# The adaLN shift as a bias per output column, in place of a term in h

## The chip, the cores and the metric

The kernel runs on one core of a Trainium2 chip. The metric is the device time of one execution in microseconds (us), median of three runs, less is better. The engines are named as in the profile: PE is TensorE, PEld its weight loads, DVE is VectorE, ACT is ScalarE, POOL is GpSimd, SP is SyncE, which issues the DMA transfers.

## What is computed

One layer of a bidirectional hybrid encoder over 2048 tokens of 1024 channels:

```python
mod = silu(c) @ ada_w + ada_b
shift, scale, gate = split(mod, 3)
h = rms_norm(x, norm_w) * (1.0 + scale) + shift
proj = h @ w_in                     # 1024 -> 3088 columns
u_a, z_a, qkv, z_b, beta_fb, alpha_fb = split(proj)
# u_a: state-space group, then a gated linear unit, times silu(z_a)
# qkv: centred conv of 5 taps, silu, gated delta rule in both directions, times silu(z_b)
out = x + gate * (concat(y_a, y_b) @ w_out)     # then a final rms_norm
```

The shift is one vector for all tokens, so `h @ w_in` is `(h - shift) @ w_in` plus one constant for each output column.

## The kernel before

Tokens lie in four blocks of 512 (b or tb), channels in eight slices of 128 (k). h is kept transposed, as two float16 halves hhi and hlo of h times a power of two; the factor that undoes it is ih. Columns of w_in are taken in jobs of 128: `order` lists four u jobs (numbers 0 to 3, NU = 4), ZA0 to ZA2, the narrow job ab (16 columns: beta and alpha), K0 to K3, Q0 to Q3, and then V0, ZA3, V1, ZB0, V2, ZB1, V3, ZB2, ZB3. A weight is split into halves wh and wl with a power of two of its own: `w_max` squares it on ScalarE with a running sum and adds that up with a matmul against ones; `w_cut` makes scale and inverse iv on VectorE (`pow2_root`), then wh on ScalarE and wl on VectorE. A product (`gemm`) of one job and one block is 24 matmuls of 512 columns, three for each k.

Both stages that the change touches are under a manual schedule: each engine gets its instructions in the order of the program text. Nothing is reordered, and an instruction that waits holds up what stands behind it on its engine.

**The start** (lines 250 to 500) makes the modulation, h and the u jobs. Scale comes first: acc is the weighted sum of eight rows blocks of ada_w, and `mod_sum` adds it up over partitions on TensorE. Block 0 of h is made without the shift, with its own factor ih0 (line 378), and the four u products of block 0 run on it, kept in four PSUM banks. Meanwhile the shift's weighted sum runs on VectorE (`shift_add`) and, for the last two rows, on GpSimd (line 412); `mod_sum(0, ...)` follows in the middle of product 3. Then `h_scale` takes a new factor from scale and shift together, and `h_part` makes block 1 of h with the shift:

```python
A.activation(out=hf, in_=src, func=AF.Identity, scale=aS[:, k:k + 1], bias=shS[:, k:k + 1])
P.tensor_scalar(out=hhi[:, k, sl], in0=hf, scalar1=1.0, scalar2=1.0, op0=ALU.mult, op1=ALU.mult)
V.tensor_tensor(out=hlo[:, k, sl], in0=hf, in1=hhi[:, k, sl], op=ALU.subtract)
```

What block 0 lacks is added to u only: 96 matmuls of one column (line 438) multiply the four u weights with the shift, in halves shh and shl, and the evacuation of block 0 gets the result as a bias. The loop over blocks 1 to 3 (line 465) interleaves the u products with the next block's h: squares and root of x, its scaling, four turns (transposes by TensorE, `h_turn`) per slot and `h_part`. In block 3 the slots for the next h are used to make block 0's h again, from xk, with the shift (line 481). There too the first projection job's weight is prepared.

**The projection jobs** (line 986 on): `job` runs four products, each followed by an evacuation by ScalarE (a z with Silu, or raw for the conv) and by `tick`, which issues what became due: taps and conv of earlier blocks, sums, turns, and a piece of `s5_side`, the state-space branch with its tables. Under the first product the next weight's Square is issued, under the second its small matmul, under the third and fourth its cut. `ab_job` runs its four blocks in four column groups of TensorE at once, and prepares K0's weight in one go behind them, with no tick between. PSUM has two banks for products (gm), three each for pt and sq. The stages behind the jobs are not touched.

Of the kernel before, what the change touches and what calls it, by code (L numbers as in the profile page):

```python
# [9 lines left out]
F32 = mybir.dt.float32  # L10
# [13 lines left out]
KT = D // 128  # L24
# [16 lines left out]
def block(ctx, tc, x, c, ada_w, ada_b, norm_w, w_in, conv_w,  # L41
# [131 lines left out]
    ih = hpool.tile([128, 1], F32, name="ih")  # L173
    cw = s5t.tile([128, 12, 5], F32, name="cw")
# [20 lines left out]
    def w_max(i):  # L195
# [5 lines left out]
        m, ma, s, iv = [sp.tile([128, 1], F32, tag=f"w{j}", name=f"w{j}", bufs=6) for j in range(4)]  # L201
        wh, wl = [pools["wp", i < NU].tile([128, KT, order[i][1]], F16, tag=t, name=t) for t in ("wh", "wl")]
        A.activation(out=wl.bitcast(BF16), in_=ws, func=AF.Square, accum_out=m)
        wprep[i] = [None, ma, s, iv, wh, wl]
# [6 lines left out]
    def w_cut(i):  # L211
# [3 lines left out]
        ps, ma, s, iv, wh, wl = wprep[i]  # L215
        ws = wraw[i]
        pow2_root(ps, ma, s, iv)
        if i >= NU:
            V.tensor_tensor(out=iv, in0=iv, in1=ih, op=ALU.mult)
# [4 lines left out]
        wprep[i] = (wh, wl, iv)  # L224
# [5 lines left out]
    def w_done(i):  # L230
        w = wprep[i][0:3]
        if i < NU:
            V.tensor_tensor(out=w[2], in0=w[2], in1=ih, op=ALU.mult)
        return w
# [15 lines left out]
    with ExitStack() as p0:  # L250
# [134 lines left out]
        ss = x_square(x1)  # L385
        first = []
        iv0 = small("iv0", NU)
# [7 lines left out]
        first.append(gemm(wprep[0], 0))  # L395
        next(cuts[2])
        next(cuts[2])
# [32 lines left out]
        for k in range(3):  # L430
            h_part(1, k, turned[k])
# [1433 lines left out]
```

## Time and profile before

| | us |
|---|---|
| median of three runs | 1396.05 (1393.25 to 1398.34) |
| the profiled execution: own time | 1399.54 |
| its span | 1397.8 |
| PE busy | 1283.2 (92%) |
| DVE busy | 1000.4 (72%) |
| POOL, ACT busy | 703.7, 672.1 |
| mean granted clock of TensorE, as a share of the full one | 0.959 |

The profile is of one execution. Busy time of PE counts overlapping matmuls, whose ends are modelled, so the step from start to start says more than the duration of a row. The full clock of TensorE is 2.4 GHz, its lower level 1.2.

### The profile page before, as it was taken

To read this page: it belongs to the slowest core of one execution; us is meant where nothing else is said; L and a number is where in the kernel's file an instruction comes from. 1 tells how busy PE (TensorE), PEld (TensorE's weight loads), DVE (VectorE), ACT (ScalarE), POOL (GpSimd) and SP (SyncE) were. 2 spreads that over 40 slices of the span, in tenths; PEclk is the share of its full clock that TensorE was granted. 3 is DMA by queue.
4 is the path that set the end of the run, shared out by engine and by line. 5 is a ranking of instruction groups with operands and counts; after the bars stand their busy time and mean duration, and the time that the engine had idled before them with its cause. 6 is when DMAs were issued, how large, how long until landed. Compare 5 with 4: busy or idle time off the path is not lost.

```text
span 1397.8 us, 26533 instructions
## 1 busy us (share of the span) xinstructions
PE 1283.2 (92%) x9936; PEld 902.9 (65%) x9936; DVE 1000.4 (72%) x2095; ACT 672.1 (48%) x1348; POOL 703.7 (50%) x680
## 2 busy tenths in 40 slices
PE   2879897898999999999998789999999988998997
PEld 2445343354665555555554679999998877887885
DVE  4636479877765899889865677888888555865664
ACT  4445321444654555344446566777666423432332
POOL 3214223655541478878731765656653235654443
PEclk9789998999999999999999899999999999999998
DMA  9445342222457434353525423444435487686533
GB/s 313 169 93 180 96 83 84 66 80 83 117 170 186 134 113 144 91 163 100 150 74 150 147 77 116 152 145 138 132 111 197 144 289 276 226 309 211 181 111 108
DMA packets 255280, 206.43 MB, mean 148 GB/s; under 512 B 88496, under 2 KB 206256, under 8 KB 255152
## 3 DMA queue, kind: packets, MB, share of 16 engines
q1 hardware_dynamic: 255152, 204.75, 47.5%
q8 instruction: 78, 1.28, 0.4%
q14 instruction: 50, 0.41, 0.1%
HBM read 133.38 MB, written 73.33 MB: 148 GB/s over the span
## 4 chain that ended last, share of the span: by engine, by line
PE 70%; DVE 16%; DMA 4%; issue 3%; ACT 2%; POOL 2%; SPq 1%; DVEq 0%; POOLq 0%; ACTq 0%
PE gm L33 38%; PE sq L33 16%; PE pt L33 12%; DVE sq L1035 3%; DVE w L510 1%; DVE tm L510 1%; DVE xs L939 1%; PE pt L1079 1%; DMA of<-o_d 1%; DVE t L510 1%; DVE wl L223 1%; PE sq L1752 1%; DMA xt<-in_x_dram 1%; DMA ay_d<-ytx 1%; DVE pb L1423 0%
## 5 line engine op out<-in xcount | busy, mean ns | idle before, releaser
L33 PE MATMUL gm<-hhi,wh 128*128 128x512 f16 (+1 forms) x784 | 294.3, 392 | 14.7 <-ACT wh L221 8.2
L33 PE MATMUL gm<-hhi,wl 128*128 128x512 f16 (+1 forms) x784 | 293.1, 390 | 8.8 <-DVE wl L223 8.8
L33 PE MATMUL gm<-hlo,wh 128*128 128x512 f16 (+1 forms) x784 | 293.3, 391 | 0.0
L33 PEld LDWEIGHTS <-wh 128*128 128x128 f16 (+1 forms) x1664 | 154.0, 101 | 200.6 <-issue 25.3
L33 PEld LDWEIGHTS <-wl 128*128 128x128 f16 (+1 forms) x832 | 79.7, 100 | 106.7 <-DVE wl L223 11.4
L1019 ACT ACTIVATE raw<-gm,w 128x512 f32<-128x512 f32 x48 | 33.1, 690 | 177.6 <-PE gm L33 177.6
L510 POOL TENSOR_TENSOR w<-w,w 128x512 f32<-128x512 f32 x32 | 50.1, 1575 | 83.3 <-DVE w L510 83.3
L33 PE MATMUL gm<-yh,gwh 128*128 128x256 f32 x256 | 80.4, 314 | 6.4 <-ACT yh L778 5.4
L1035 DVE SCALAR_TENSOR_TENSOR sq<-raw,cw,sq 128x512 f32<-128x512 f32 x96 | 72.6, 756 | 3.4
L33 PE MATMUL gm<-yl,gwh 128*128 128x256 f32 x256 | 73.7, 288 | 0.7 <-POOL yl L779 0.7
L1774 POOL TENSOR_TENSOR r<-r,xt 128x512 f32<-128x512 f32 x32 | 41.4, 1295 | 63.5 <-DVE r L1773 31.0
L33 PE MATMUL gm<-yh,gwl 128*128 128x256 f32 x256 | 72.9, 285 | 0.0
L1035 DVE SCALAR_TENSOR_TENSOR sq<-raw,cw,cv 128x512 f32<-128x512 f32 x48 | 50.7, 1057 | 29.3 <-ACT cv L1027 28.7
L1444 ACT ACTIVATE Y<-pt 128x512 f16<-128x512 f32 x96 | 58.0, 604 | 27.1 <-PE pt L33 26.4
L33 PE MATMUL sq<-S,kq 128*128 128x128 f32 x480 | 64.1, 287 | 0.0
L33 PEld LDWEIGHTS sq<-S,kq 128*128 128x128 f32 x480 | 61.7, 201 | 2.0
L1005 ACT ACTIVATE z<-gm,w 128x512 f32<-128x512 f32 x32 | 22.0, 688 | 84.6 <-PE gm L33 49.7
L1423 DVE CAST_PREDICATED pb<-msk,pt 128x512 f16<-128x512 int8 x80 | 56.9, 714 | 6.6 <-PE pt L33 5.4
L939 DVE TENSOR_TENSOR_SCAN xs<-c,w 128x255 f32<-128x255 f32 x64 | 61.1, 1013 | 0.6 <-POOL w L510 0.6
L33 PE MATMUL pt<-Y,nh 128*128 128x64 f16 (+1 forms) x896 | 56.5, 198 | 5.4 <-DVE Y L1431 5.1
L320 POOL TENSOR_SCALAR hhi<-hf 128x512 f16<-128x512 f32 x32 | 30.0, 957 | 55.0 <-ACT hf L318 47.9
L1445 ACT ACTIVATE YT<-pt 128x512 f16<-128x512 f32 x96 | 57.3, 597 | 0.0
(456 smaller groups left out, 3529.8 us busy)
## 6 DMA issues: line engine op xcount, KB each, us to landing
xt<-in_x_dram SPq DMA_DIRECT2D x25, 512.0 KB
ws<-in_w_in_dram SPq DMA_DIRECT2D x24, 512.0 KB
aw<-in_ada_w_dram SPq DMA_DIRECT2D x24, 512.0 KB
kq<-kT_d SPq DMA_DIRECT2D x32, 256.0 KB
kq<-qT_d SPq DMA_DIRECT2D x32, 256.0 KB
kt<-kt_d SPq DMA_DIRECT2D x32, 256.0 KB
vt<-vt_d SPq DMA_DIRECT2D x32, 256.0 KB
out_dram<-r SPq DMA_DIRECT2D x16, 512.0 KB
```

Source lines behind the costliest of these rows:

```text
L33: nc.tensor.matmul(out, lhsT, rhs, start=start, stop=stop)
L223: V.scalar_tensor_tensor(out=wl, in0=ws, scalar=s, in1=wh, op0=ALU.mult, op1=ALU.subtract)
L320: P.tensor_scalar(out=hhi[:, k, sl], in0=hf, scalar1=1.0, scalar2=1.0, op0=ALU.mult, op1=ALU.mult)
L510: (e or V).tensor_tensor(out=o, in0=a, in1=b, op=op)
L939: V.tensor_tensor_scan(out=o, data0=m1, data1=v, initial=0.0, op0=ALU.mult, op1=ALU.add)
L1005: A.activation(out=z, in_=ps, func=AF.Silu, scale=iv)
L1019: A.activation(out=raw[:, 2 + tb * 512:2 + (tb + 1) * 512], in_=ps, func=AF.Copy, scale=iv)
L1035: V.scalar_tensor_tensor(out=cv if j == 4 else ps, in0=raw[:, o + j:o + j + 512], scalar=cw[:, i12, j:j + 1], in1=cv if j == 1 else ps, op ...
L1423: V.copy_predicated(out=cols(PB[d][li], b, d), mask=mb, data=pp.rearrange("p t (n b) -> p t n b", b=b))
L1444: A.activation(out=cols(Y[d], b, d), in_=pa.rearrange("p t (n b) -> p t n b", b=b), func=AF.Copy)
L1445: A.activation(out=cols(YT[d], b, 1 - d), in_=pb.rearrange("p t (n b) -> p t n b", b=b), func=AF.Copy)
L1774: P.tensor_tensor(out=r[:, ns], in0=r[:, ns], in1=xt[:, ns], op=ALU.add)
```

## The change

The shift is kept out of h altogether, in every block. `h_part` becomes two instructions, hhi straight from the source on ScalarE and hlo on VectorE, with no use of GpSimd; block 0 isn't made again, and h's factor comes from scale alone, so it is there from the beginning. Each job instead gets a bias per column, from `w_bias`: 24 matmuls of one column of the weight's halves with the shift's (three for each k), and an evacuation that undoes weight's and shift's factors (ib, a second product beside iv). In a job it is issued behind the first product and ahead of its evacuation; in ab it is 96 matmuls, 24 for each of the four column groups, and four evacuations.

In the start the six u products of block 0 and of jobs 0 and 1 in block 1 are evacuated without a bias into xk (`u_raw`). The shift is summed up between them; squares, root and scaling of block 2 come ahead of its last step. The four u jobs' biases follow product (1,1), and GpSimd adds them to the six kept u (`u_add`), which are stored then.

```diff
+
+    ish = hpool.tile([128, 1], F32, name="ish")
+    sh = [hpool.tile([128, KT], F16, name=n) for n in ("shh", "shl")]
...
@@ -212,26 +215,33 @@
 
         if i >= len(order):
             return
-        ps, ma, s, iv, wh, wl = wprep[i]
+        ps, ma, s, iv, ib, wh, wl = wprep[i]
         ws = wraw[i]
         pow2_root(ps, ma, s, iv)
         if i >= NU:
+            V.tensor_tensor(out=ib, in0=iv, in1=ish, op=ALU.mult)
             V.tensor_tensor(out=iv, in0=iv, in1=ih, op=ALU.mult)
         yield
         A.activation(out=wh, in_=ws, func=AF.Copy, scale=s)
         yield
         V.scalar_tensor_tensor(out=wl, in0=ws, scalar=s, in1=wh, op0=ALU.mult, op1=ALU.subtract)
-        wprep[i] = (wh, wl, iv)
+        wprep[i] = (wh, wl, iv, ib)
 
     def whole(g):
         for _ in g:
             pass
 
...
-    def w_done(i):
-        w = wprep[i][0:3]
-        if i < NU:
-            V.tensor_tensor(out=w[2], in0=w[2], in1=ih, op=ALU.mult)
-        return w
+    def w_bias(w, n, rows=(0,)):
+
+        ps = bank("pt")
+        for k in range(KT):
+            for a, b, j in ((0, 0, 0), (0, 1, 1), (1, 0, 2)):
+                for r in rows:
+                    mm(nc, ps[r:r + n, 0:1], w[a][:, k, :], sh[b][:, k:k + 1], k + j == 0, k == KT - 1 and j == 2)
+        wb = sp.tile([128, 1], F32, tag="wb", name="wb", bufs=NU)
+        for r in rows:
+            A.activation(out=wb[r:r + n], in_=ps[r:r + n, 0:1], func=AF.Copy, scale=w[3][r:r + n])
+        return wb
...
         def h_part(b, k, src):
-            hf = hp.tile([128, 512], F32, tag="hf", name="hf", bufs=4)
-            A.activation(out=hf, in_=src, func=AF.Identity, scale=aS[:, k:k + 1], bias=shS[:, k:k + 1])
             sl = slice(b * 512, (b + 1) * 512)
-            P.tensor_scalar(out=hhi[:, k, sl], in0=hf, scalar1=1.0, scalar2=1.0, op0=ALU.mult, op1=ALU.mult)
-            V.tensor_tensor(out=hlo[:, k, sl], in0=hf, in1=hhi[:, k, sl], op=ALU.subtract)
+            A.activation(out=hhi[:, k, sl], in_=src, func=AF.Copy, scale=aS[:, k:k + 1])
+            V.scalar_tensor_tensor(out=hlo[:, k, sl], in0=src, scalar=aS[:, k:k + 1], in1=hhi[:, k, sl],
+                                   op0=ALU.mult, op1=ALU.subtract)
...
-        s_0, ih0, s_h = [small(n) for n in ("s_0", "ih0", "s_h")]
-        h_scale(bd, s_0, ih0, "h0")
-        aS0, aS, shS = [small(n, KT) for n in ("aS0", "aS", "shS")]
-        V.tensor_scalar(out=aS0, in0=aT, scalar1=s_0, scalar2=None, op0=ALU.mult)
+        s_h, s_s = small("s_h"), small("s_s")
+        h_scale(bd, s_h, ih, "h")
+        aS, shS = small("aS", KT), small("shS", KT)
+        V.tensor_scalar(out=aS, in0=aT, scalar1=s_h, scalar2=None, op0=ALU.mult)
         cuts = {i: w_cut(i) for i in range(1, NU)}
-
         for k in range(KT):
-            A.activation(out=hhi[:, k, 0:512], in_=xk[:, k], func=AF.Copy, scale=aS0[:, k:k + 1])
-            V.scalar_tensor_tensor(out=hlo[:, k, 0:512], in0=xk[:, k], scalar=aS0[:, k:k + 1], in1=hhi[:, k, 0:512],
-                                   op0=ALU.mult, op1=ALU.subtract)
+            h_part(0, k, xk[:, k])
...
-        ss = x_square(x1)
-        first = []
-        iv0 = small("iv0", NU)
+        raws = {}
...
-        first.append(gemm(wprep[0], 0))
-        next(cuts[2])
-        next(cuts[2])
-        shift_add(0, 1)
+        def u_raw(b, ct):
+
+            if b == 0:
+                iv, ib = wprep[ct][2:4]
+                V.tensor_copy(out=ib, in_=iv)
+                V.tensor_tensor(out=iv, in0=iv, in1=ih, op=ALU.mult)
+            u_out(b, ct, gemm(wprep[ct], b), None)
+
+        def u_add(b, ct):
+            ur = raws.pop((b, ct))
+            P.tensor_scalar(out=ur, in0=ur, scalar1=ub[ct], scalar2=1.0, op0=ALU.add, op1=ALU.mult)
+            u_store(b, ct, ur)
+
+        def u_store(b, ct, ur):
+            nc.sync.dma_start(out=u_d[ct * 128:(ct + 1) * 128, :, b * 64:(b + 1) * 64], in_=ur)
+
+        def u_out(b, ct, ps, bias):
+
+            ur = (xk[:, 4 * b + ct].rearrange("p (t r) -> p t r", t=T) if bias is None else
+                  up.tile([128, T, 64], F32, tag="u", name="u"))
+            ps = ps.rearrange("p (r t) -> p t r", t=T)
+            if bias is None:
+                A.activation(out=ur, in_=ps, func=AF.Copy, scale=wprep[ct][2])
+                raws[b, ct] = ur
+            else:
+                A.activation(out=ur, in_=ps, func=AF.Identity, scale=wprep[ct][2], bias=bias)
+                u_store(b, ct, ur)
+
         whole(cuts[2])
-        first.append(gemm(wprep[1], 0))
-        whole(w_max(3))
+        ss = x_square(x1)
+        u_raw(0, 0)
+        mx = w_max(3)
+        next(mx)
         rs = x_root(ss)
         for j in range(4):
             x_scale(x1, rs, j, (A, P)[j % 2])
-        next(cuts[3])
-        next(cuts[3])
+        u_raw(0, 1)
+        whole(mx)
+        whole(cuts[3])
...
+        u_raw(0, 2)
+        shift_add(0, 1)
+        for k in range(0, 4):
+            h_part(1, k, h_turn(x1, k, turns[k % 2]))
         shift_add(2, 3)
-        whole(cuts[3])
+        u_raw(0, 3)
+        for k in range(4, KT):
+            h_part(1, k, h_turn(x1, k, turns[k % 2]))
+        xs_ = {2: x_load(2)}
         shift_add(4, 5)
 
...
-        first.append(gemm(wprep[2], 0, "sq"))
-        turned = [h_turn(x1, k, t) for k, t in enumerate(("pt", "pt", "sq"))]
-        first.append(bank("sq"))
-        gemm_part(first[3], wprep[3], 0, range(4))
+        u_raw(1, 0)
+        ss = x_square(xs_[2])
         mod_sum(0, [acc, aws[6]])
-        gemm_part(first[3], wprep[3], 0, range(4, KT))
-        xs_ = {2: x_load(2)}
+        rs = x_root(ss)
+        for j in range(4):
+            x_scale(xs_[2], rs, j, V)
...
-        V.tensor_tensor(out=bd, in0=bd, in1=bs_, op=ALU.add)
-        h_scale(bd, s_h, ih, "h")
-        V.tensor_scalar(out=aS, in0=aT, scalar1=s_h, scalar2=None, op0=ALU.mult)
-        V.tensor_scalar(out=shS, in0=modc[:, 0:8], scalar1=s_h, scalar2=None, op0=ALU.mult)
-        sh = [hp.tile([128, KT], F16, name=n, bufs=1) for n in ("shh", "shl")]
+        h_scale(bs_, s_s, ish, "s")
+        V.tensor_scalar(out=shS, in0=modc[:, 0:8], scalar1=s_s, scalar2=None, op0=ALU.mult)
         V.tensor_copy(out=sh[0], in_=shS)
         V.tensor_tensor(out=sh[1], in0=shS, in1=sh[0], op=ALU.subtract)
-        for k in range(3):
-            h_part(1, k, turned[k])
+        u_raw(1, 1)
+        ub = []
         for ct in range(NU):
-            V.tensor_tensor(out=iv0[:, ct:ct + 1], in0=wprep[ct][2], in1=ih0, op=ALU.mult)
...
-        uw = [w_done(ct) for ct in range(NU)]
-        for ct in range(NU):
-            for k in range(KT):
-                for w, h_, n in ((0, 0, 0), (0, 1, 1), (1, 0, 2)):
-                    mm(nc, pmod[:, 16 + ct:17 + ct], uw[ct][w][:, k, :], sh[h_][:, k:k + 1], k + n == 0,
-                       k == KT - 1 and n == 2)
-        for k in range(3, KT):
-            h_part(1, k, h_turn(x1, k, ("sq", "pt")[k % 2]))
-        ub = small("ub", NU)
-        for ct in range(NU):
-            V.tensor_scalar(out=ub[:, ct:ct + 1], in0=pmod[:, 16 + ct:17 + ct], scalar1=uw[ct][2], scalar2=None,
-                            op0=ALU.mult)
-
-        def u_out(b, ct, ps, iv, **kw):
-            ur = up.tile([128, T, 64], F32, tag="u", name="u")
-            A.activation(out=ur, in_=ps.rearrange("p (r t) -> p t r", t=T),
-                         func=AF.Identity if kw else AF.Copy, scale=iv, **kw)
-            nc.sync.dma_start(out=u_d[ct * 128:(ct + 1) * 128, :, b * 64:(b + 1) * 64], in_=ur)
-
-        for ct in range(NU):
-            u_out(0, ct, first[ct], iv0[:, ct:ct + 1], bias=ub[:, ct:ct + 1])
+
+            ib = wprep[ct][3]
+            V.tensor_tensor(out=ib, in0=ib, in1=ish, op=ALU.mult)
+            ub.append(w_bias(wprep[ct], 128))
+        for b, ct in ((0, 0), (0, 1), (0, 2), (0, 3), (1, 0), (1, 1)):
...
-                u_out(b, ct, gemm(uw[ct], b), uw[ct][2])
+                if b > 1 or ct > 1:
+                    u_out(b, ct, gemm(wprep[ct], b), ub[ct])
                 if b < NB - 1:
-                    if ct == 0:
+                    if ct == 0 and b == 1:
+                        xs_[3] = x_load(3)
+                        w_dma(NU)
+                    elif ct == 0:
                         rs = x_root(x_square(xs_[b + 1]))
-                        if b == 1:
-                            xs_[3] = x_load(3)
-                            w_dma(NU)
...
-                elif ct < 2:
-                    for k in range(4 * ct, 4 * ct + 4):
-                        h_part(0, k, xk[:, k])
...
     def job(i, evac):
-        w = w_done(i)
+        w = wprep[i]
         for tb in range(NB):
             ps = gemm(w, tb)
-            evac(tb, ps, w[2])
+            if tb == 0:
+                wb = w_bias(w, 128)
+            evac(tb, ps, w[2], wb)
             if tb == 0:
                 w_dma(i + 2)
                 mx, cut = w_max(i + 1), w_cut(i + 1)
@@ -1000,9 +1019,9 @@
             tick()
...
+        def evac(tb, ps, iv, wb):
             z = tp.tile([128, 512], F32, tag="z", name="z", bufs=3)
-            A.activation(out=z, in_=ps, func=AF.Silu, scale=iv)
+            A.activation(out=z, in_=ps, func=AF.Silu, scale=iv, bias=wb)
...
+        def evac(tb, ps, iv, wb):
+            A.activation(out=raw[:, 2 + tb * 512:2 + (tb + 1) * 512], in_=ps, func=AF.Identity, scale=iv, bias=wb)
```

## Rows read from the trace of the kernel before

**Rows 1.** The page: busy time; groups, xcount | busy, mean ns | idle before.

```profile
PE 1283.2 (92%) x9936; PEld 902.9 (65%) x9936; DVE 1000.4 (72%) x2095; ACT 672.1 (48%) x1348; POOL 703.7 (50%) x680
...
L33 PEld LDWEIGHTS <-wh 128*128 128x128 f16 (+1 forms) x1664 | 154.0, 101 | 200.6 <-issue 25.3
...
L320 POOL TENSOR_SCALAR hhi<-hf 128x512 f16<-128x512 f32 x32 | 30.0, 957 | 55.0 <-ACT hf L318 47.9 <-issue 6.8
```

**Rows 2.** Windows: busy us of each engine, granted clock, DMA share, GB/s.

```profile
220.00:240.00 20.00, 11.90 (x63) 5.36 (x60) 19.62 (x49) 3.13 (x9) 12.43 (x11) 0.83 0.22 67
...
400.00:500.00 100.00, 99.79 (x613) 58.10 (x612) 72.47 (x134) 52.04 (x93) 35.15 (x37) 1.00 0.59 158
```

**Rows 3.** The chain that ended last, in the start: start, us, what.

```profile
85.45 17.80 PE gm L33 x72
...
104.22 0.44 PE pt L313 x4
...
105.09 5.18 PE gm L33 x24
...
136.34 10.37 PE gm L33 x48
...
151.92 11.73 PE gm L33 x48
```

**Rows 4.** Timeline of PE: start, us, instruction, [idle before <-releaser].

```profile
85.45 0.61 PE L33 MATMUL gm<-hhi,wh 128*128 128x512 f16 x1 [6.47 <-ACT u L449]
...
151.33 0.59 PE L33 MATMUL pt<-w,ones 128*128 128x1 f32 x2 [4.63 <-ACT wl L203]
```

**Rows 5.** Timeline of ACT, PE and DVE around the job ab.

```profile
240.67 1.07 ACT L203 ACTIVATE wl<-ws 128x1024 bf16<-128x1024 f32 x1
...
248.21 0.39 PE L33 MATMUL gm<-hhi,wl 128*16 128x512 f16 x4
...
248.94 0.16 DVE L143 TENSOR_SCALAR w<-pt 128x1 int32<-128x1 int32 x1 [5.42 <-PE pt L33]
```

**Rows 6.** Timeline of PE from the turns of block 1 to the last bias product.

```profile
58.16 1.04 PE L313 MATMUL pt<-ident,xt 128*128 128x128 f32 x8
...
62.77 0.38 PE L33 MATMUL pt<-ones,acc 128*128 128x1 f32 x2 [0.18 <-DVE acc L279]
...
66.88 0.59 PE L33 MATMUL sq<-hhi,wh 128*128 128x512 f16 x1
...
71.95 0.21 PE L33 MATMUL pt<-shh,wh 128*128 128x1 f16 x1
...
74.42 0.16 PE L33 MATMUL pt<-shh,wl 128*128 128x1 f16 x1
```

**Rows 7.** Timeline of DVE and ACT: the shift's low half; squares, root and scaling of block 2.

```profile
69.57 0.17 DVE L429 TENSOR_TENSOR shl<-shS,shh 128x8 f16<-128x8 f32 x1
...
93.56 1.05 ACT L294 ACTIVATE jk<-xt 128x1024 bf16<-128x1024 f32 x1
...
98.27 0.17 DVE L299 TENSOR_SCALAR ss<-ss 128x4 f32<-128x4 f32 x1 [13.31 <-ACT jk L294]
...
100.66 2.74 DVE L307 TENSOR_SCALAR xt<-xt,rs 128x1024 f32<-128x1024 f32 x4
```

**Rows 8.** Timeline of SP's queue: the conv weights.

```profile
89.99 7.88 SPq L461 DMA_DIRECT2D cw<-in_conv_w_dram  x5
```

**Rows 9.** Groups of small instructions, 150 to 760 us.

```profile
L860 ACT ACTIVATE l<-sq 128x16 f32<-128x16 f32 x8 | 1.5, 184 | 0.0
...
L1118 ACT ACTIVATE ab<-gm,w 16x512 f32<-16x512 f32 x4 | 2.7, 680 | 2.2 <-DVE ab L1116 2.2
...
L219 DVE TENSOR_TENSOR w<-w,ih 128x1 f32<-128x1 f32 x21 | 7.7, 368 | 0.7
```

**Rows 10.** Timeline of DVE: two sums of the shift, beside GpSimd's.

```profile
53.49 3.42 DVE L279 SCALAR_TENSOR_TENSOR acc<-aw,sc,acc 128x1024 f32<-128x1024 f32 x2
```

**Rows 11.** The chain that ended last, in the jobs.

```profile
525.21 3.20 DVE xs L939 x4
```

More of the change, by code (lines that the diff above doesn't have):

```diff
@@ L200, in w_max @@
         ws = wraw[i]
-        m, ma, s, iv = [sp.tile([128, 1], F32, tag=f"w{j}", name=f"w{j}", bufs=6) for j in range(4)]
+        m, ma, s, iv, ib = [sp.tile([128, 1], F32, tag=f"w{j}", name=f"w{j}", bufs=6) for j in range(5)]
         wh, wl = [pools["wp", i < NU].tile([128, KT, order[i][1]], F16, tag=t, name=t) for t in ("wh", "wl")]
         A.activation(out=wl.bitcast(BF16), in_=ws, func=AF.Square, accum_out=m)
-        wprep[i] = [None, ma, s, iv, wh, wl]
+        wprep[i] = [None, ma, s, iv, ib, wh, wl]
         yield
@@ L404, in block @@
             x_scale(x1, rs, j, (A, P)[j % 2])
-        next(cuts[3])
-        next(cuts[3])
+        u_raw(0, 1)
+        whole(mx)
+        whole(cuts[3])
+        turns = ("pt", "sq")
+        u_raw(0, 2)
+        shift_add(0, 1)
+        for k in range(0, 4):
+            h_part(1, k, h_turn(x1, k, turns[k % 2]))
         shift_add(2, 3)
-        whole(cuts[3])
+        u_raw(0, 3)
+        for k in range(4, KT):
+            h_part(1, k, h_turn(x1, k, turns[k % 2]))
+        xs_ = {2: x_load(2)}
         shift_add(4, 5)
@@ L453, in block @@
-        for ct in range(NU):
-            u_out(0, ct, first[ct], iv0[:, ct:ct + 1], bias=ub[:, ct:ct + 1])
+            ib = wprep[ct][3]
+            V.tensor_tensor(out=ib, in0=ib, in1=ish, op=ALU.mult)
+            ub.append(w_bias(wprep[ct], 128))
+        for b, ct in ((0, 0), (0, 1), (0, 2), (0, 3), (1, 0), (1, 1)):
+            u_add(b, ct)
         pada.close()
@@ L1002, in z_job @@
     def z_job(i, dst):
-        def evac(tb, ps, iv):
+        def evac(tb, ps, iv, wb):
             z = tp.tile([128, 512], F32, tag="z", name="z", bufs=3)
-            A.activation(out=z, in_=ps, func=AF.Silu, scale=iv)
+            A.activation(out=z, in_=ps, func=AF.Silu, scale=iv, bias=wb)
             nc.sync.dma_start(out=dst[:, tb * 512:(tb + 1) * 512], in_=z)
@@ L1016, in conv_job @@
             ss, rk = [sp.tile([128, NCH], F32, tag=t, name=t, bufs=2) for t in ("kss", "rk")]
-        def evac(tb, ps, iv):
-            A.activation(out=raw[:, 2 + tb * 512:2 + (tb + 1) * 512], in_=ps, func=AF.Copy, scale=iv)
+        def evac(tb, ps, iv, wb):
+            A.activation(out=raw[:, 2 + tb * 512:2 + (tb + 1) * 512], in_=ps, func=AF.Identity, scale=iv, bias=wb)
             if tb:
@@ L1103, in ab_job @@
     def ab_job(i):
-        wh, wl, iv = w_done(i)
+        wh, wl, iv = wprep[i][0:3]
         ps = bank("gm")
@@ L1111, in ab_job @@
                        k == 0 and n == 0, k == KT - 1 and n == 2)
+        wb = w_bias(wprep[i], 16, [32 * j for j in range(NB)])
         w_dma(i + 2)
@@ L1117, in ab_job @@
         for j in range(NB):
-            A.activation(out=ab[32 * j:32 * j + 16], in_=ps[32 * j:32 * j + 16], func=AF.Copy,
-                         scale=iv[32 * j:32 * j + 16])
+            A.activation(out=ab[32 * j:32 * j + 16], in_=ps[32 * j:32 * j + 16], func=AF.Identity,
+                         scale=iv[32 * j:32 * j + 16], bias=wb[32 * j:32 * j + 16])
         later(2, lambda: ab_turn(ab))
```

## The prediction

> **What bounds the kernel now.** I read the page first: TensorE is busy for 92% of the span, and no other engine comes near [rows 1]. That share is an average, so I took stages next. Between 400 and 500 us TensorE works for 99.79 of 100 us at clock 1.00; between 220 and 240 it is VectorE that is full, 19.62 of 20 us, with TensorE at 11.90 [rows 2]. The start shows neither: there the chain of waits tells more. Block 0's products are done, but block 1's h needs the shift, so the chain leaves TensorE for ScalarE, GpSimd and VectorE until a product starts at 85.45. The chain's first three products then take 17.80 us where one takes 5.18 [rows 3], 2.26 more than three: the engine had stood still for 6.47 us [rows 4] and comes back at the low clock. A second hole lies in the last block. ScalarE does block 0's h over again there, and only then the Square on which the next weight's scale rests; TensorE waits 4.63 us [rows 4]. From 146.71 (136.34 + 10.37) to 163.65 (151.92 + 11.73) it does two products, 10.36 us of work, in 16.94 [rows 3].
>
> So there are two kinds of stage: a start with holes, and projection jobs, most of them full on TensorE, where an added instruction is added time. Between them lie some 80 us that VectorE's tables fill, with one gap of 5.42 us at the narrow job ab [rows 5].
>
> **The change: the start.** Block 1's h no longer needs the shift. Up to 58.16 us TensorE's order is as before. Then come four turns of 0.44 each [rows 3] to 59.9, product 3 to 65.1, four turns to 66.8, product (1,0) to 72.0, the modulation's sum (62.77 to 66.88, 4.1 us) to 76.1, and product (1,1). Before, that sum ended at the low clock and the next 12 matmuls took 5.07 us, 66.88 to 71.95, instead of 2.6 [rows 6]; I let this happen again, and (1,1) ends at 83.8.
>
> The bias products wait for the shift's two halves, and in the new order these stand on VectorE behind the root and scaling of block 2. (1,0) is evacuated by 72.7; four Squares take 4.7 (93.56 to 98.27), to 77.4; root and scaling 5.1 (98.27 to 103.40), to 82.5; from the sum's end to the low half it was 2.9 (66.88 to 69.74) [rows 6, 7], less two operations and the wait that go, 2.3, to 84.8. The chain over ScalarE and VectorE thus ends last, 1.0 us after product (1,1). The 96 bias matmuls of the four u jobs are those of before, 71.95 to 74.42, 2.5 us [rows 6], to 87.3, and ten products are left. Before, ten were left at 85.45 + 17.80 - 5.18 = 98.07. **Gain 10.8 us**, or 8.5 if TensorE leaves this point at the low clock, 2.26 again.
>
> hlo from PSUM (eight) and the shift's weighted sums stand on VectorE from 57 to some 73 us; the sums have to be ready when (1,0) ends at 72, and a us there costs nothing, because the Squares end later.
>
> In the last block the second pass over block 0 goes. What stays before TensorE can go on is an evacuation of 0.65, a Square with its read (1.18, a quarter of the 4.7) and two small matmuls: 2.3 us with hand-overs, where 16.94 - 10.36 = 6.6 were lost. **Gain 4.3 us.** The work that leaves GpSimd and VectorE is worth nothing beyond that.
>
> The six late additions of the bias on GpSimd (bounds: nothing, and the 0.96 us of its 128x512 conversion [rows 1]; I take 0.8) run beside products. SyncE's queue is behind them: six u stores wait for them, and behind those stand the gate's load, the five conv loads (7.88 us of issue [rows 8]) and block 3 of x. I get the last issue for x near 103 and its arrival near 108; its Squares can start near 107 and the fourth near 110.5. Hidden, with 2 to 3 us left; every us beyond is lost. Start in all: 15.1 us, 12.8 with the low clock; **I take 14**.
>
> **The jobs.** Each gets 24 matmuls of one column, a small evacuation (wb) and, on VectorE, a product of two columns (ib). 96 in 2.5 us is 26 ns each, 0.62 us per job [rows 6].
>
> [...] The row is that of 96 load-and-multiply pairs in a run. [...]
>
> From K1 on (281 us) sixteen jobs have TensorE as their bound: 16 x 0.62 = **9.9 us**. The first two, ZA0 and ZA1, lie on TensorE's part of the chain: 0.9, since the side work's loads go out behind the first evacuation, and 0.6, **1.5**. ZA2 and K0 lie under VectorE's tables and cost nothing, or 0.62 each if that cover goes.
>
> ab has no cover. Its bias has four column groups, 96 matmuls. Behind them in ScalarE's queue stand four small evacuations and then the Square of K0's weight, which before ran at 240.67, beneath ab's own products; VectorE sat idle for 5.42 us until 248.94 for what follows that Square [rows 5]. The matmuls: at least a quarter of 96 x 26 ns, 0.6, since the four groups can run together as ab's own do (x4 in [rows 5]); at most 96 x 101 ns, 9.7, if each waited for a weight load [rows 1]; I take the 2.5 of [rows 6], the nearest row. The evacuations: 4 x 0.18 by the narrow one of 128x16, at most 4 x 0.68 [rows 9]. The Square with its read 1.2. **4.5 us**, between 2.5 and 13.6.
>
> ib: nearest is the identical product on line 219, 0.37 us on average [rows 9], alone about half of that; five lie where VectorE decides, at 0.25, **1.2**. Elsewhere TensorE hides them. A bias on the wide evacuations makes ScalarE wait for wb, about 0.9 us behind the first product; the bank it empties is wanted four us later, and the Square queued behind is wanted a product later: nothing. A bank for the bias products is the one that pt has left at that point: nothing, or up to the 0.7 us of a VectorE operation if its reader is late.
>
> Jobs: 9.9 + 1.5 + 4.5 + 1.2 = 17.1. **Net +3.1 us.** The profiled execution's own time is 1399.54 us (span 1397.8 and 1.74 around it), which makes 1402.6. It lay 3.5 above the median of the three runs; from the median, 1396.05, I get 1399.2. What a measurement of this kernel can tell from no change is 0.3%, 4.2 us, so the forecast is *no change*: a start that is won and a row of jobs that pays it back.
>
> **Rivals.**
> *Slower: the shift comes late.* VectorE's queue is full from 57 to 73 us, and beside GpSimd's work its weighted sums took 1.71 us each (3.42 for two [rows 10]). Should that push the shift past 84.8, all ten products move with it; from 1.1 us on the kernel is slower by more than 0.3%. With 3 us and the low clock after it, the start is worth 12.8 - 3 = 9.8: net +7.3, 1403.4. For it: no slack on this chain by my own sum. Against: the sums are not wanted before 82.
> *Faster: the bias products hide.* The chain runs over VectorE in a part of the late jobs, as at 525 us [rows 11], and TensorE's records overlap, so its 99.79 may hold gaps. If eight of the sixteen jobs pay (5.0) and ab's matmuls run four at a time (2.5), the jobs cost 10.2; with the full 15.1 of the start, -4.9, 1391.2. Against: no TensorE idle is shown there.
> *Slower by far: each pair is paced by its weight load.* A load of 128 columns lasts 101 ns [rows 1]. Then 18 jobs pay 1.8 more each and ab 7.2: +39.6, 1439. The bias products of [rows 6] speak against it, at a quarter of that. [...]
>
> **Numbers.** The forecast (net between -4.2 and +4.2) 0.50; late shift 0.38; paced by loads 0.02; hidden bias 0.10. So faster 0.10, same 0.50, slower 0.40. The low end: the full start against jobs with 14 paying and ab at 3.7, between its bound and my value (8.7 + 1.5 + 3.7 + 1.2 = 15.1), net 0, less a measurement's 4.2: 1392. The high end: the late shift with ZA2 and K0 uncovered and ab 2 dearer, 20.3 - 9.8 = 10.5: 1406.5.
>
> **What would show it.** The last u product ends near 149.6 instead of 163.65; TensorE waits 1 us before the bias products, near 85, and some 2 instead of 4.63 before the weight's scale. In the jobs, 480 more one-column matmuls on 128 columns, 26 ns apart; VectorE's wait at ab 10 instead of 5.42. I am wrong in the start if the bias products begin after 86 or block 3's Squares wait for x, and in the jobs if the stretch behind the last u product grows by less than 13 or more than 21 us.

## The result and the profile after

The changed kernel took **1402.63 us** (median of 5 executions, 1401.91 to 1406.70), the kernel before 1396.64 beside it: ratio **1.0050, 95% interval 1.0034 to 1.0065**. Measured again later with another group of kernels it took 1403.17, ratio 1.0052 (1.0038 to 1.0067). So it is slower by half a per cent, 7 us by the ratios. Below, a ratio is turned into us with 1 % = 13.97 us, the kernel before at 1397.

The profiled execution took 1402.61 us, span 1400.9. From its page, then the window that answers to the second of [rows 2] and the one behind it:

```profile
PE 1295.8 (92%) x10512; PEld 915.0 (65%) x10512; DVE 988.8 (71%) x2106; ACT 678.5 (48%) x1368; POOL 677.4 (48%) x654
```

```profile
400.00:500.00 100.00, 99.69 (x684) 57.88 (x683) 71.70 (x133) 52.02 (x91) 34.48 (x36) 1.00 0.57 157
500.00:600.00 100.00, 98.72 (x627) 54.62 (x626) 93.33 (x126) 50.30 (x81) 79.66 (x68) 1.00 0.40 120
```

There are 576 more matmuls (10512 against 9936): 20 jobs x 24, and 96 at ab. TensorE was full in the jobs before and still is.

The start, from the timeline of PE and the chain that ended last (the last two rows are the chain's, the last u products and then the gate's):

```profile
72.43 0.38 PE L33 MATMUL pt<-ones,acc 128*128 128x1 f32 x2 [0.41 <-DVE acc L289]
...
84.60 0.18 PE L33 MATMUL pt<-shh,wh 128*128 128x1 f16 x1 [1.57 <-DVE shh L463]
...
141.83 0.38 PE L33 MATMUL pt<-w,ones 128*128 128x1 f32 x2 [1.96 <-ACT wl L206]
```

```profile
142.21 10.38 PE gm L33 x48
152.59 1.72 PE pt L33 x4
```

The holes of 6.47 and 4.63 us [rows 4] are down to 1.57 and 1.96, and the last u product ends at 152.59 instead of 163.65. This execution has won 11.1 us there, and gives it all back, and 3.1 more, behind it: the stretch behind the last u product grows by 14.1 us, which lies between the 13 and 21 of the prediction.

Around ab, from the timelines of PE, ACT and DVE:

```profile
238.34 0.17 PE L33 MATMUL pt<-shh,wh 128*16 128x1 f16 x4
...
239.36 1.09 ACT L243 ACTIVATE wb<-pt,w 16x1 f32<-16x1 f32 x4 [11.81 <-PE pt L33]
240.47 1.06 ACT L206 ACTIVATE wl<-ws 128x1024 bf16<-128x1024 f32 x1
...
242.09 0.16 DVE L143 TENSOR_SCALAR w<-pt 128x1 int32<-128x1 int32 x1 [8.28 <-PE pt L33]
```

The Square of K0's weight (L206), which ran beneath ab's products before [rows 5], now begins behind them: 2.1 us after the start of the bias products, which is the first row. VectorE waits 8.28 us where it waited 5.42.

**A ledger of the jobs.** Every product of the 20 wide jobs is evacuated once by ScalarE, 80 evacuations (z or raw) in the same order in every kernel here. Their start in each trace, minus that in the first trace of the kernel before, says where time is won or lost. Columns: number 4 (188.36 us before, first job ZA0 done), 11 (224.90, ahead of ab), 13 (256.96, K0's first), 24 (342.25, K2 done), 76 (740.05, all but the last job done); then what the 13 jobs between 24 and 76 cost against the kernel before.

| kernel | 4 | 11 | 13 | 24 | 76 | 24 to 76 |
|---|---|---|---|---|---|---|
| before, second profile | 5.13 | 5.12 | 5.29 | 3.35 | 3.38 | 0.03 |
| changed | -9.80 | -8.64 | -3.65 | -6.99 | 2.77 | **9.76** |
| changed, second profile | -6.83 | -5.67 | -0.52 | -3.86 | 5.94 | **9.80** |
| no bias in jobs | -6.51 | -6.52 | -6.23 | -7.81 | -7.80 | 0.01 |
| bias matmuls left out | -7.57 | -7.63 | -3.60 | -5.82 | -2.88 | 2.94 |
| bias matmuls twice | -7.02 | -4.66 | -0.12 | -4.55 | 13.37 | 17.92 |
| ab's bias later | -4.96 | -3.80 | 0.61 | -4.12 | 5.68 | 9.80 |
| x earlier | -10.38 | -9.22 | -4.50 | -7.84 | 1.95 | 9.79 |
| three changes of order | -11.21 | -10.06 | -11.67 | -14.55 | -4.73 | 9.82 |
| the same, 16 matmuls | -13.67 | -12.92 | -14.92 | -17.47 | -9.91 | 7.56 |
| before + early Square | -2.44 | -2.44 | -2.16 | -3.96 | -3.94 | 0.02 |
| the same + ab's order | -1.76 | -1.77 | -5.57 | -3.49 | -3.47 | 0.02 |

The reader is to see two things. The last column repeats to 0.06 us wherever the code of the jobs is the same, so a difference in it is cause, not chance. The first column doesn't: the start of one and the same code differs by 5 us between two executions. In the later one the sum of the modulation waits for VectorE, and the granted clock between 56 and 112 us is 0.76 instead of 0.85, which over 56 us is those 5 us (timeline of PE, second profile of the kernel before):

```profile
64.11 0.38 PE L33 MATMUL pt<-ones,acc 128*128 128x1 f32 x2 [1.75 <-DVE acc L279]
```

Behind number 80 stand some 630 us of code that no kernel here touches; they took 632 to 639 us. Times of the whole are therefore compared by several executions of each kernel, not by one pair of traces.

### The profile page after: what moved, and what is told of

It reads as the page before. It is cut to its first block, busy times and chain, and to the rows that moved or that the text cites. A ratio compares the mean times of both kernels' runs of the same rounds, so it can differ in the third digit from the quotient of the medians.

```text
span 1400.9 us, 27663 instructions
## 1 busy us (share of the span) xinstructions
PE 1295.8 (92%) x10512; PEld 915.0 (65%) x10512; DVE 988.8 (71%) x2106; ACT 678.5 (48%) x1368; POOL 677.4 (48%) x654
## 4 chain that ended last, share of the span: by engine, by line
PE 68%; DVE 13%; ACT 3%; DMA 2%; issue 2%; SPq 1%; POOL 1%; DVEq 0%; ACTq 0%; POOLq 0%
PE gm L33 36%; PE sq L33 17%; PE pt L33 13%; DVE sq L1054 2%; PE pt L1098 1%; DMA y<-ya_d 1%; DVE w L527 1%; DVE tm L527 1%; DVE YT L1456 1%; DVE pb L1443 1%; PE sq L1772 1%; DVE xs L956 0%; DVE t L527 0%; DVE r L1804 0%; DMA xt<-in_w_out_dram 0%
## 5 line engine op out<-in xcount | busy, mean ns | idle before, releaser
L33 PE MATMUL gm<-hhi,wl 128*128 128x512 f16 (+1 forms) x800 | 300.3, 391 | 10.5 <-DVE wl L227 10.5
L33 PE MATMUL gm<-hhi,wh 128*128 128x512 f16 (+1 forms) x800 | 301.6, 392 | 3.5 <-ACT wh L225 3.5
L33 PE MATMUL gm<-hlo,wh 128*128 128x512 f16 (+1 forms) x800 | 300.4, 391 | 0.0
L33 PEld LDWEIGHTS <-wh 128*128 128x128 f16 (+1 forms) x2048 | 168.6, 99 | 195.0 <-issue 26.2
L33 PEld LDWEIGHTS <-wl 128*128 128x128 f16 (+1 forms) x1024 | 93.0, 99 | 108.2 <-DVE wl L227 12.4
L1038 ACT ACTIVATE raw<-gm,wb,w 128x512 f32<-128x512 f32 x48 | 37.4, 779 | 123.8 <-PE gm L33 123.4
L1054 DVE SCALAR_TENSOR_TENSOR sq<-raw,cw,cv 128x512 f32<-128x512 f32 x48 | 47.0, 979 | 36.6 <-ACT cv L1046 35.9
L227 DVE SCALAR_TENSOR_TENSOR wl<-ws,w,wh 128x1024 f16<-128x1024 f32 (+1 forms) x25 | 32.6, 1305 | 34.6 <-ACT wh L225 34.6
L33 PEld LDWEIGHTS <-nh 128*128 128x128 f16 x1024 | 48.1, 98 | 13.1 <-issue 6.2
```

The lines of the kernel that those rows point to most:

```text
L33: nc.tensor.matmul(out, lhsT, rhs, start=start, stop=stop)
L227: V.scalar_tensor_tensor(out=wl, in0=ws, scalar=s, in1=wh, op0=ALU.mult, op1=ALU.subtract)
L1038: A.activation(out=raw[:, 2 + tb * 512:2 + (tb + 1) * 512], in_=ps, func=AF.Identity, scale=iv, bias=wb)
L1054: V.scalar_tensor_tensor(out=cv if j == 4 else ps, in0=raw[:, o + j:o + j + 512], scalar=cw[:, i12, j:j + 1], in1=cv if j == 1 else ps, op ...
```

## The experiments

**What the start is worth.** The bias is left out of all jobs behind the u jobs:

```diff
-            if tb == 0:
-                wb = w_bias(w, 128)
+            wb = None
             evac(tb, ps, w[2], wb)         # evacuations: Copy and Silu without a bias, as before
...
-        wb = w_bias(wprep[i], 16, [32 * j for j in range(NB)])      # at ab; ib isn't made either
```

> The changed kernel with the bias left out of all jobs behind the u jobs (no bias products, no wb, no ib, evacuations as before; the modulation's shift is therefore missing from those outputs). What is left of the change is the start. Theory (the start gains 11 us and the jobs pay 14 to 17 back): 10 to 12 us under the kernel before, about 1385.5, and 14 to 17 under the changed kernel. Rival (the stretch that VectorE's tables fill, 165 to 280 us, swallows part of an earlier start whatever the jobs do): only 4 to 7 us under the kernel before, 1390 to 1392.

Measured 1387.55, ratio 0.9931 (0.9917 to 0.9944): 9.6 us under the kernel before, and 16.6 under the changed one. Nearer to the theory's 10 than to the rival's 7; in the ledger nothing of it is swallowed by VectorE's tables (-6.5 to -7.8 across them). The start's gain is real, and less than the 14 us of the prediction.

**The price of the matmuls**, once with none and once with two sets:

```diff
-                wb = w_bias(w, 128)
+                wb = w_bias(w, 128, src=ps)    # no matmuls; wb read from the product's first column
```
```diff
-                wb = w_bias(w, 128)
+                wb = w_bias(w, 128, times=2)   # all 24 twice
```

> The changed kernel with the 24 bias matmuls left out of each of the 20 wide jobs; wb is evacuated from the first column of the product instead, so ScalarE's and VectorE's share of the change stays (the outputs of these jobs get a wrong bias). Theory (the jobs pay for TensorE's time): 16 jobs x 0.62 = 9.9 us under the changed kernel, up to 12 with the first jobs: 1391 to 1393. Rival (they pay for the wait on wb, for evacuations with a bias, 0.78 for 0.69 us, and for ib on VectorE): at most 3 us under the changed kernel, 1400 or more.

> The changed kernel with the 24 bias matmuls of each of the 20 wide jobs done twice (the second pass starts the sum afresh, so the result is the same). Theory: 16 x 0.62 to 20 x 0.62, 10 to 12.5 us over the changed kernel, 1413 to 1415. Rival (the matmuls hide in gaps of TensorE's row, the price is elsewhere): 0 to 3 us over. Second rival (a pair is paced by its weight load of 101 ns): 16 x 24 x 0.101 = 39 us over.

Without them 1393.81, ratio 0.9976 (0.9962 to 0.9991): 10.3 us under the changed kernel, as the theory has it. With two sets 1411.39, ratio 1.0099 (1.0085 to 1.0113): 6.8 us over it, below the expected 10 to 12.5, but far from the 39 of loads that pace each pair. The ledger is sharper: the second set costs 17.92 - 9.78 = 8.1 us in 13 jobs, **0.63 us per job**, and the first 9.78 - 2.94 = 6.8. (The Trainium skill, "TensorE: Matmul & The Clock Gate", section Back-to-back issue gap, has an issue floor of about 25 ns for a matmul of 1 to 64 columns. The trace agrees: 0.63 us for 24 is 26 ns each, with the weight load.) The first costs less because, with no matmuls at all, another wait shows that they otherwise cover in part. From the timeline of PE without them:

```profile
533.87 1.21 PE L33 MATMUL sq<-uT,tt 128*128 128x256 f32 x4 [0.53 <-DVE w L527]
...
544.49 1.95 PE L33 MATMUL sq<-uT,bpt 128*64 128x256 f32 x16 [1.77 <-DVE w L527]
```

and from that of the changed kernel, whose window of 500 to 600 us above has the hole in its 98.72:

```profile
546.45 1.95 PE L33 MATMUL sq<-uT,bpt 128*64 128x256 f32 x16 [1.27 <-DVE w L527]
```

Near 545 us VectorE is nearly as full as TensorE (93.33 of the 100 us from 500 on), and what the change adds to it (ib) or makes it wait for comes out as a wait of TensorE: 2.3 us without the matmuls, 1.3 with one set, none with two, nor with no bias at all. Which of VectorE's additions it is wasn't taken apart.

**ab.** Its bias behind the Square and the small matmuls:

```diff
-        wb = w_bias(wprep[i], 16, [32 * j for j in range(NB)])
         w_dma(i + 2)
         whole(w_max(i + 1))
+        wb = w_bias(wprep[i], 16, [32 * j for j in range(NB)])
         whole(w_cut(i + 1))
```

> The changed kernel with the bias of job ab moved behind the Square of K0's weight and its two small matmuls; the same result. Theory (at ab the 96 matmuls and four small evacuations stand ahead of that Square, and VectorE, which decides here, waits for what follows it): the Square starts 0.84 + 1.09 us earlier plus hand-overs, 1.9 to 2.5 us under the changed kernel, 1400 to 1400.7. Rival (VectorE has tables to do in that time, its wait ends later whatever the Square does): no change, within 0.7 us of the changed kernel.

Measured 1402.24, ratio 1.0028 (1.0018 to 1.0037): 3 us under the changed kernel by the ratios, 0.4 to 0.9 by the medians, so open by the times alone. In the ledger ab (11 to 13) costs 4.41 instead of 4.99, only 0.6 less. The trace says why: the Square now comes early, but wb stands ahead of the weight's cut in ScalarE's queue instead (timeline of ACT):

```profile
244.70 1.09 ACT L243 ACTIVATE wb<-pt,w 16x1 f32<-16x1 f32 x4 [9.98 <-PE pt L33]
245.81 1.15 ACT L225 ACTIVATE wh<-ws,w 128x1024 f16<-128x1024 f32 x1
```

**The load of x.** This kernel's trace also showed a loss that the first trace had only at 0.7 us. From its timelines of ACT and PE:

```profile
112.43 1.06 ACT L304 ACTIVATE jk<-xt 128x1024 bf16<-128x1024 f32 x1 [3.72 <-DMA xt<-in_x_dram]
```

```profile
121.38 0.33 PE L323 MATMUL pt<-ident,xt 128*128 128x128 f32 x1 [3.12 <-DVE xt L317]
```

TensorE lost 3.8 us there to block 3's x, which arrived late; in the six traces of this start 0.7 to 3.8. So the load was put ahead of the late additions and their stores, and the changed kernel measured beside it once more:

```diff
+        xs_[3] = x_load(3)
         for b, ct in ((0, 0), (0, 1), (0, 2), (0, 3), (1, 0), (1, 1)):
             u_add(b, ct)
...
                     if ct == 0 and b == 1:
-                        xs_[3] = x_load(3)
                         w_dma(NU)
```

> The changed kernel once more, unaltered, for a second profile and times beside the others of this group. Theory (the change costs 4 to 7 us: a start of -10 and jobs of +14 to +17): 1.003 to 1.005 of the kernel before. In the profile the Squares of block 3 should again wait for x, by 1 to 5 us in all. Rival (the first measurement of +6 was chance, and the pair of traces with +3 is right): 1.002 or less.

> The changed kernel with the load of x for block 3 issued ahead of the six late additions of the bias and their stores; the same result. Theory (the six stores, the gate's load and the conv loads stand before x in SyncE's queue, the reserve that was counted on is used up, and TensorE loses between 0.7 and 4 us in the last block by it): the Squares of block 3 wait for nothing, 1 to 3 us under the changed kernel. Rival (what delays the Squares is the load on the memory in that stretch, or the loss is made good further on): no change, within 0.7 us.

The unaltered kernel came out at 1403.17 (ratio 1.0052), so the first measurement stands. With the early load 1398.31, ratio 1.0013 (1.0000 to 1.0026): **5.4 us under it**, more than the 1 to 3 expected. From its timeline of ACT, the first and the last Square, with no wait on any of the four:

```profile
108.81 1.04 ACT L304 ACTIVATE jk<-xt 128x1024 bf16<-128x1024 f32 x1
...
112.34 1.06 ACT L304 ACTIVATE jk<-xt 128x1024 bf16<-128x1024 f32 x1
```

From block 1's first turn to ZA0's first evacuation it took 101.9 us, against 102.5 to 105.9, 104.4 on average, in the six traces with the late load: 2.5 us, of which TensorE's waits for x are 1.6 on average. In the trace that lost 3.8 the granted clock between 112 and 135 us is 0.85, too, where it is 1.00 in the others. The rest of the 5.4 no trace shows; each of the two ratios is known to some 2 us either way, so part of it can be chance.

**The kernel before, with parts of the gain.** First the Square that made the hole of 4.63 us:

```diff
                 elif ct < 2:
+                    if ct == 0:
+                        mx = w_max(NU)
+                        next(mx)               # the Square, ahead of the second pass over block 0
                     for k in range(4 * ct, 4 * ct + 4):
                         h_part(0, k, xk[:, k])
...
-                        whole(w_max(NU))
+                        whole(mx)
```

> The kernel before, with one edit: in the last block the Square of the next weight is issued ahead of the second pass over block 0 (its two small matmuls stay where they were); the same result. Theory (the last block's 4.63 us of waiting come from that Square's place behind the pass, not from the pass as such): 3.5 to 5 us under the kernel before, 1393. Rival (the second pass itself holds TensorE up, since the first job needs its last h): at most 1 us under.

1391.39, ratio 0.9960 (0.9946 to 0.9974): **5.6 us under**, a little over the 3.5 to 5 expected. The second pass stays, so it was the Square's place behind it that cost most of this. The wait that is late next, on PE, is the gate's, a third of the old one:

```profile
160.62 1.98 PE L33 MATMUL pt<-accg,ones 128*128 128x512 f32 x4 [1.46 <-DVE accg L279]
```

The changed kernel, which has no second pass, doesn't wait there (152.59 above); whether the pass makes VectorE late for the gate no run takes apart. The 3.2 us less of waiting and the 1.37 us that the low clock behind the hole had cost (11.73 us for 10.36 [rows 3]; here the granted clock from 160 to 170 us is 1.00) make some 4.5 of the 5.6.

Then block 1's high half on ScalarE, since GpSimd's next instruction came 7 us after its reduction:

```diff
+            if b == 1:
+                A.activation(out=hhi[:, k, sl], in_=hf, func=AF.Copy)
+            else:
                 P.tensor_scalar(out=hhi[:, k, sl], in0=hf, ...)
```

> The kernel before with the early Square and, for block 1 alone, the high half of h converted on ScalarE instead of GpSimd; the same result. Theory (block 1's h is late in the kernel before not only for the shift, but because GpSimd's next instruction comes 7 us after its reduction starts, at 75.21 where its input lies there from 70): the first product of block 1 starts near 80 instead of 85.45, and with the Square 8 to 10 us go, 1387 to 1389: most of what the start's new order wins, with nothing to pay in the jobs. Rival (the gap on GpSimd is only how its spans are recorded, or ScalarE's 16 passes take as long): no more than the early Square alone.

1392.31, ratio 0.9965 (0.9952 to 0.9977): no more than the Square alone. My theory fell, and the second half of the rival held. The first product of block 1, with the early Square alone and with both, from the timelines of PE:

```profile
87.79 0.61 PE L33 MATMUL gm<-hhi,wh 128*128 128x512 f16 x1 [6.32 <-ACT u L449]
```

```profile
85.55 0.59 PE L33 MATMUL gm<-hhi,wh 128*128 128x512 f16 x1 [5.22 <-ACT u L452]
```

It starts 2.2 us earlier, not 5. In both, TensorE is released by the evacuation of a bank (u), and that waits for a bias which VectorE makes behind the last low half of block 1's h. ScalarE's sixteen passes last from 71.40 to 83.83 us, with one wait of 1.59, so that this last low half can't start before 83.87.

**Both kernels with the waits of order gone**, and a second profile of the kernel before:

```diff
 # in the last block
+                if b == NB - 1 and ct == 0:
+                    mx = w_max(NU)
+                    next(mx)
 # in ab_job
+        mx, cut = w_max(i + 1), w_cut(i + 1)
+        next(mx)
         for k in range(KT):
             ...                                # ab's products
+            if k == 3:
+                whole(mx)
+                whole(cut)
+        wb = w_bias(...)                       # only in the changed kernel
-        whole(w_max(i + 1))
-        whole(w_cut(i + 1))
```

> The kernel before once more, unaltered, for a second profile. Theory (the pair of traces shows a difference of only 3 us because the first profiled execution of the kernel before was 2 to 3 us slow in stretches that the change doesn't touch, ahead of 57 us or behind 761 us): a time of 1396 to 1398, and the stretch from the first job's first evacuation to the last job's last one equal to the first profile's, 590.62 us, within 0.5. Rival (the first job's place varies inside the changed stretch): that stretch differs by more than 1 us.

> The changed kernel with three changes of order; the same result: x of block 3 loaded ahead of the late additions; the Square of the first job's weight issued one product earlier, in the last block; at ab the Square and the cut of K0's weight issued ahead of ab's own products, with ab's bias behind them. Theory (what is left of the start's holes, 1 to 3 us for x and 2.0 for the Square, and of ab's 5 us are waits made by order alone): from the early load alone at 1398.3, another 2 for the Square and 4 to 5 at ab: 1391 to 1393, under the kernel before. Rival (VectorE's tables decide up to 330 us and swallow what ab gives): 1396 or more.

> The kernel before with the early Square in the last block and, at ab, the Square and the cut of K0's weight ahead of ab's products; the same result. Theory (VectorE's wait of 4 to 5 us at ab lies on the path, since VectorE decides from there to 330 us): 3 to 5 us under the early Square alone, 1387 to 1388. Rival (that wait is made good in the tables behind it): 1391, as with the early Square alone.

The changed kernel with early x, early Square and ab's order: **1390.73, ratio 0.9946 (0.9928 to 0.9963), 7.5 us under the kernel before**, a little under the 1391 to 1393 expected. At ab VectorE waits 2.21 us instead of 8.28:

```profile
234.81 0.16 DVE L143 TENSOR_SCALAR w<-pt 128x1 int32<-128x1 int32 x1 [2.21 <-PE pt L33]
```

and what the ledger gains there (+4.99 becomes -1.61) it keeps. The kernel before with the same order: 1392.64, ratio 0.9968 (0.9952 to 0.9985), nothing beyond its early Square, where 3 to 5 us were expected. It too gains 3.8 us at ab, and loses 4.2 three evacuations later, where TensorE now waits for the next weight's cut:

```profile
272.89 0.61 PE L33 MATMUL gm<-hhi,wh 128*128 128x512 f16 x1 [3.76 <-ACT wh L221]
```

So it isn't VectorE's tables that swallowed it, as the rival had it, but a new wait.

The change itself is therefore not shown to be worth anything beyond these orders: the intervals of the changed kernel in its new order (0.9946) and of the kernel before with the early Square alone (0.9960) overlap.

The second profile of the kernel before (one execution, 1398.24 us, span 1396.5) missed my expectation: its stretch of jobs is 588.87 us, 1.75 shorter than in the first, mostly between 321 and 335 us. Its start was 5.1 us later and what follows the jobs 4.7 shorter than in the first. The forecast's +3.1 and the first pair of traces' +3.1 agree in part by chance.

**Sixteen matmuls instead of 24.** The two halves of the shift become two columns of one matmul with wh, summed while they are evacuated:

```diff
-            for a, b, j in ((0, 0, 0), (0, 1, 1), (1, 0, 2)):
+            for a, q in ((0, 2), (1, 1)):
                 for r in rows:
-                    mm(nc, ps[r:r + n, 0:1], w[a][:, k, :], sh[b][:, k:k + 1], ...)
+                    mm(nc, ps[r:r + n, 0:q], w[a][:, k, :], sh2[:, k, 0:q], ...)
...
-            A.activation(out=wb[r:r + n], in_=ps[r:r + n, 0:1], func=AF.Copy, scale=w[3][r:r + n])
+            A.activation(out=wc[r:r + n], in_=ps[r:r + n, 0:2], func=AF.Copy, scale=w[3][r:r + n], accum_out=wb[r:r + n])
```

> The kernel with the three changes of order, and the bias products as 16 matmuls instead of 24 (the two halves of the shift as two columns of one matmul, summed as the bias is evacuated); the same result to within rounding. Theory (TensorE's time for the bias products is what the late jobs pay): 8 x 0.026 us x 14 to 20 jobs, 2.9 to 4.2 us under the one with 24 matmuls. Rival (it is the wait on wb, which now has an extra read behind it): the same or slower.

1391.20, ratio 0.9945 (0.9927 to 0.9963), the same as with 24. In the ledger the 13 jobs cost 7.56 instead of 9.82, 0.17 us less per job where 8 x 0.026 = 0.21 were expected; the intervals, 2.5 us either way, can't show a gain of 2 to 3 us, and in this execution what follows the jobs took 639 us, the longest of all. Whether the whole gains stays open.

## Why the prediction came out as it did

The forecast was no change, +3.1 us, 1399.2; measured was +6 by the medians and +7 by the ratios, slower by more than the 0.3% that can be told apart, and within the range of 1392 to 1406.5. The shape (a start that is won, jobs that pay it back) held; two sizes in the start were off. One of the prediction's own signs of being wrong came true: block 3's Squares waited for x.

*The bias products of the u jobs* began at 84.60 (forecast 84.8) after a wait of 1.57 us (1.0), and ended at 87.26 (87.3). In this trace the shift was not late, so the rival that was to make the kernel slower did not happen here; that its +7.3 is the size measured is chance. It is not quite absent, though: the working has the weighted sums in time when (1,0) ends, and in eight of the nine traces of this start the modulation's sum waits for them, 0.40 to 1.79 us. Counted from block 1's first turn (58.01 here), the bias products begin after 26.6 us, as forecast, to 27.5 in eight traces, but after 29.5 in the second profile of the changed kernel (its timeline of PE):

```profile
74.86 0.38 PE L33 MATMUL pt<-ones,acc 128*128 128x1 f32 x2 [1.79 <-DVE acc L289]
```

*The low clock behind them* came: the granted clock is 0.70 between 88 and 96 us, and the turns behind the product that starts at 87.26 begin at 95.19, after 7.9 us for 5.18. The working had this as "8.5 if TensorE leaves this point at the low clock" and took half of it; it should have taken it whole. In other traces of this start the low stretch lies in part before the bias products, but from 66 to 100 us the mean granted clock is 0.85 in seven of the nine, 5.1 us, against the 4.7 of both terms of the working (2.5 in (1,1) and 2.26).

*The last block's Square*: the hole is 1.96 us (forecast 2), and from its beginning, 141.83 - 1.96 = 139.87, to the last u product's end at 152.59 it is 12.72 us, which is 2.34 over two products (2.3). The 4.3 us held, and as the early Square shows, they were to be had without the change (5.6 by its ratio).

*The step that failed is the transfer:* "I get the last issue for x near 103 and its arrival near 108 ... Hidden, with 2 to 3 us left". From the timelines of POOL and of SP's queue:

```profile
83.10 0.41 POOL L338 PARTITION_ALL_REDUCE sma<-sm  x1 [14.93 <-DVE sm L337]
90.47 4.03 POOL L409 TENSOR_SCALAR xk<-xk,wb 128x512 f32<-128x512 f32 x6 [6.96 <-issue]
```

```profile
91.17 5.76 SPq L413 DMA_DIRECT2D u_d<-xk  x6
96.98 1.13 SPq L478 DMA_DIRECT2D gate<-in_ada_b_dram  x1
98.17 6.68 SPq L480 DMA_DIRECT2D cw<-in_conv_w_dram  x5
104.96 2.30 SPq L296 DMA_DIRECT2D xt<-in_x_dram  x4
```

The first bias lay ready near 86, but GpSimd's first addition begins at 90.47, seven us after its reduction. Everything behind it on SyncE moves by that, x is issued from 104.96 to 107.26, and the Squares wait. The queue was modelled, the engine at its head not. No run takes GpSimd's wait away by itself; what was tried is x ahead of that queue, and it won 5.4 us, of which the traces show 0.7 to 3.8 as waits of TensorE. Start by the times: -9.6, for a forecast of -14.

*The jobs' matmuls* were priced right: 0.62 us forecast, 0.63 by the second set. From the view of the tile wb (ns: shortest, median, longest), the small evacuation:

```profile
L243 ACT ACTIVATE wb<-pt,w x28: 251/261/263, 85.6 to 750.7; 128x1 f32<-128x1 f32 x24, 16x1 f32<-16x1 f32 x4
```

Between numbers 24 and 76 the bound was indeed TensorE's: 13 jobs at 9.8 us in all, 8.1 by the matmuls and most of the rest the 1.3 us wait at 546. Over K0, K1 and K2 the forecast was too dear: there the changed kernel gains against the first trace (-3.65 to -6.99, 3.3 us). Of this 1.6 to 1.9 are a loss of the first trace alone, since the kernel before gains them too in its second profile and with the early Square, and so does the kernel without a bias. The rest says that the bias costs nothing there: VectorE still holds TensorE up in the changed kernel, and its cover reaches further than K0 (timeline of PE):

```profile
320.36 0.66 PE L1098 MATMUL pt<-ident,cv 128*128 128x128 f32 x4 [1.46 <-DVE w L143]
```

*ab*: 4.5 us forecast. VectorE's wait grew by 8.28 - 5.42 = 2.9, and from 11 to 24 the changed kernel loses 1.7 against before and 2.9 against the kernel without a bias. The matmuls took the low bound, 0.84 us with the evacuation's start, not the 2.5 that I took: the four column groups ran at once. All jobs, from 4 to the last evacuation: 13.2 us in the first trace, 14.5 against the kernel without a bias (-1.3), for 17.1 forecast, of which 0.9 lies ahead of number 4; by the ratios 16.6.

So start and jobs were both put too high, the start by 4 us and the jobs by 0.5 (ratios) to 4 (traces), and the errors cancelled in part. That the bias on the wide evacuations costs nothing held in the sense that no wait on it shows between 285 us and the end of the jobs; the two rivals of hidden products and of products paced by their loads fell with the two sets.

## What to carry to other kernels

Before work is moved for the sake of a hole, look whether the hole is only one of order: here one Square issued earlier, without the change, won 5.6 us, and the change that won more in the start lost it again, most of it as the 0.63 us in each of the jobs that follow. A step that is moved ahead of a queue has to be followed to the head of that queue, including what its first engine is doing at that moment; the reserve of 2 to 3 us that was counted on here was used up by 4.5 us at the engine ahead of the queue. And to price an addition, double it as well as leave it out: the two prices differ where the addition hides another wait.

## What the runs showed of the hardware

GpSimd was not to be had for some 7 us after its all-reduce over the partitions, though the row of it has 0.41 us. In the kernel before (timeline of POOL):

```profile
67.95 0.41 POOL L329 PARTITION_ALL_REDUCE hma<-hm  x1 [8.84 <-DVE hm L328]
75.21 3.23 POOL L320 TENSOR_SCALAR hhi<-hf 128x512 f16<-128x512 f32 x4 [6.85 <-issue]
```

In the nine traces of the changed start the idle time behind it was 6.89 to 7.39 us, in eight of them put down to nothing that the profile shows. (Spans on GpSimd are rough in the profile; VectorE went on with the result at 68.40, 0.45 us after the row's start.) The Trainium skill, "GPSIMD Engine Reference", section Instruction dispatch, has the first call to freshly loaded code cost about 6 us with no visible instruction; the size is near, but whether that is the cause no run here shows.

A matmul of one column with a fresh load of 128 columns ran every 25 to 26 ns also in the jobs, between products (0.60 us for 24 in the chain of the changed kernel, the row below). In four column groups they ran four at a time, 96 within 1 us (from 238.34 to the evacuation at 239.36 above):

```profile
159.49 0.60 PE pt L33 x24
```

A bias given as a column made the wide evacuation 89 ns longer, 779 for 690 ns. The Trainium skill, "ScalarE: Activation LUTs", section What ACT_TABLE_LOAD costs, has some 93 ns for each such operand, and the trace agrees.
